# A decoder segment whose residual moves from features to tokens on the partitions

## The chip, the cores and the metric

One core of a Trainium2 chip runs the whole program. The metric is device time in microseconds (us). Five engines run side by side, each in the order of its own list of instructions, which is fixed before the run: TensorE (PE, matrix products), VectorE (DVE), ScalarE (ACT), GpSimd (POOL) and SyncE (SP). They wait for one another through semaphores. PE writes to PSUM only; DVE and ACT read PSUM and write SBUF. DMA queues bring the weights from memory.

## The reference, cut to what matters

Two layers over 256 tokens with 2048 features, all float32. Layer 0 mixes tokens with a gated recurrence (HGRN2), layer 1 with differential attention. Everything else is matrix products around one residual stream `x`:

```python
for i in range(2):
    h = rms_norm(x, ln_mix[i])
    if i == 0:
        q, f, v, g = split(h @ a_w_in)            # 2048 -> 4 * 2048
        x = x + (rms_norm(hgrn2(q, f, v), a_onorm) * silu(g)) @ a_w_out
    else:
        q = rms_norm(h @ b_w_q, q_norm)
        x = x + (rms_norm(diff_attention(q, k, v), b_subln) * c) @ b_w_out
    h = rms_norm(x, ln_mlp[i])
    x = x + square(relu(h @ mlp_up[i])) @ mlp_down[i]          # 2048 -> 8192 -> 2048
    gate = sigmoid(rms_norm(x, ln_ple[i]) @ ple_gate[i])
    x = x + gate * (p[i] @ ple_proj[i])                        # p[i]: 256 tokens, 256 features
    if i == 0:
        hk = rms_norm(x, kv_norm)
        k, v = rms_norm(hk @ w_k, k_norm), hk @ w_v
```

`rms_norm(x, gain)` divides each token's features by the root of their mean square and multiplies by a gain for each feature.

## The kernel before, in words

**Weights.** All weights stream through once, as 872 chunks of 256 rows x 512 columns (512 KB). `chunk` (lines 91 to 98) starts the transfer on SP's queue (four buffers `raw`), casts it on ACT to the first part `hi` (line 96), and subtracts on DVE to get the second part `lo` (line 97), three buffers each. A product in nearly full precision is made of three products of such parts: first by first, first by second, second by first.

**Two forms of product.** `group_b` (lines 119 to 131) makes 512 output features with the weights stationary: the activations, features on the partitions, are streamed with both their parts side by side, 2 x 256 tokens. For each 128x128 block of weights, `hi` meets 512 columns (line 114) and `lo` meets 256 columns (line 116): 16 matmuls a chunk. The result has features on the partitions and tokens along them, in two halves that are added afterwards; a group takes two of the three PSUM buffers `mm`, each two banks. `group_a` (lines 133 to 149) makes 512 output features with the tokens stationary: a 128-feature x 128-token block of the activations is loaded, and 512 columns of weights are streamed. That is 12 matmuls of 512 columns a chunk (lines 143 to 145), the result has tokens on the partitions, and a group takes one PSUM buffer. Before the change only the two value projections use `group_a`.

**Loops.** A matrix of 2048 x 2048 is four groups of eight chunks. The MLP (`mlp`, lines 518 to 543) goes in four quarters: four groups up (2048 inputs to 2048 hidden features), then four groups down from those into the residual.

**The residual.** `x` is 128 partitions x 16 blocks of features x 256 tokens: features on the partitions. After a group of the output or down projections, `add_x` (lines 242 to 245) adds both halves of each pair of blocks into it on DVE: four additions of 128x512 a group. `Norm` (lines 152 to 200) reads it: `split` multiplies each block by its gain (ACT, line 161) and forms the second part (DVE, line 162), `square` squares it on ACT and adds the squares on DVE, and `finish` sums over the partitions with a product with ones (line 189) and takes the inverse root. The scale for each token, `r`, is a row that every partition holds; for the value projections it is also turned into a column, by products with a unit vector (line 197). The scale is applied after the product that reads the norm.

**Gate and embedding.** `ple` computes the gate group by group with `group_b`, adds the halves, multiplies by `r`, takes the sigmoid in five steps, multiplies by the embedding's product `pp` and adds to `x` (lines 546 to 561). In layer 1 the last 512 features come in four blocks of 128, so that less is left after the last matmul. `Embed` makes `pp` with `group_b` from a single chunk a group: at the start for layer 0, in the second quarter of the MLP for layer 1.

**Order.** The Python code lists the instructions; side work stands in generators (`gens`), and `pump` takes one step of each after every chunk of weights. A planner of the language then fixes the order on each engine by its own costs of instructions and buffers, before the run: it takes what is ready by its own reckoning, first what was listed first. Side work of a norm is therefore two or three chunks behind the group it belongs to.

Of the kernel before, what the change touches and what calls it, by code (L numbers as in the profile page):

```python
# [14 lines left out]
ALU = mybir.AluOpType  # L15
# [13 lines left out]
# chunks of weights between a query projection and the first use of its heads  # L29
# [3 lines left out]
# columns of the packed small parameters  # L33
# [6 lines left out]
def kernel(ctx: ExitStack, tc: tile.TileContext, a):  # L40
# [32 lines left out]
    # side work in steps, one step of each after every chunk of weights  # L73
# [34 lines left out]
    def mm_b(ps, hi, lo, rhs, pair, k0, first, last):  # L108
        """out[features, 0:T] + out[features, T:2T] += w^T x, weights stationary"""
# [9 lines left out]
    def group_b(wsrc, g, rhs, evac, pump=None, c0=0, nch=NCH):  # L119
        """four blocks of features, in two pairs; the second starts once two chunks of the first are done"""  # L120
# [12 lines left out]
    def group_a(wsrc, g, xs, rcol, dst, pump=None):  # L133
        """dst[tokens, 512 features], tokens stationary"""
        ps = mm.tile([P, 2, CW], F32, tag="mm", name="mmps")
        for c in range(NCH):
            hi, lo = chunk(wsrc[g, c])
            for tt in range(2):
                ts = slice(tt * P, (tt + 1) * P)
                for k in range(KCS):  # L140
                    kc = c * KCS + k
                    st, en = kc == 0, kc == KC - 1
# [9 lines left out]
    class Norm:  # L152
        def __init__(self, src, outs):
            self.src, self.outs = src, outs
            self.ss = ev.tile([P, T], F32, tag="ss", name="ss", bufs=2)

        def split(self, g, outs=None, half=(0, 4)):
            for xs, col in outs or self.outs:
                for m in range(4 * g + half[0], 4 * g + half[1]):
                    gain = sml[:, col + m:col + m + 1]  # L160
                    nc.scalar.activation(xs[:, m, 0, :], self.src[:, m], AF.Copy, scale=gain)  # L161
                    nc.vector.scalar_tensor_tensor(xs[:, m, 1, :], self.src[:, m], gain,  # L162
                                                   xs[:, m, 0, :].bitcast(F32), ALU.mult, ALU.subtract)
# [12 lines left out]
        def spread(self, g, box=None, col=False):  # L176
            """split and square a group step by step, and, for the last one, put the scales into box"""
            for o in self.outs:
                for half in ((0, 2), (2, 4)):
                    self.split(g, [o], half)  # L180
                    yield
            self.square(g)
            yield
            if box is not None:
                yield from self.finish(box, col)

        def finish(self, box, col=False):
# [5 lines left out]
            if col:  # L193
                yield
                pc = sm.tile([P, 512], F32, tag="sm", name="smps")
                for tt in range(2):
                    nc.tensor.matmul(pc[:, 2 * tt:2 * tt + 2], r[:, tt * P:(tt + 1) * P], e0, start=True, stop=True)
                rc = ev.tile([P, 2, 2], F32, tag="rc", name="rc", bufs=2)
                nc.vector.tensor_copy(rc, pc[:, :4].rearrange("p (a b) -> p a b", a=2))
                box.append(rc)  # L200
# [11 lines left out]
    def col_sums(h):  # L212
        """sums over the partitions, on every partition"""
# [9 lines left out]
    def sigmoid(out, z, tmp):  # L223
        """1 / (1 + exp(-z)) as exp(min(z, 0) - ln(1 + exp(-|z|))), for z of any size"""
# [6 lines left out]
    def halves(ps, out):  # L231
        """out = both partial products of some feature blocks"""
# [9 lines left out]
    def add_x(m, ps):  # L242
        xm = x[:, m:m + 2]
        nc.vector.tensor_tensor(xm, ps[:, :, 0:T], xm, ALU.add)  # L244
        nc.vector.tensor_tensor(xm, ps[:, :, T:2 * T], xm, ALU.add)  # L245

    class Embed:
        """p[i] @ ple_proj[i], a group of features at a time"""
        def __init__(self, i, praw, pt):
            self.i, self.pt = i, pt  # L250
            self.pp = pq.tile([P, KC, T], F32, tag="pq", name="pp")
# [23 lines left out]
    nrm = Norm(xa, [(xs, C_MIX[0])])  # L275
# [4 lines left out]
    def start():  # L280
# [4 lines left out]
        yield from nrm.finish(RR, True)  # L285
# [3 lines left out]
    # lower bounds of the forget gates: softmax over the layers, first entry  # L289
# [524 lines left out]
```

## Time and profile before

| | us |
|---|---|
| median of 3 runs | 2550.68 |
| lowest and highest | 2545.85, 2551.82 |
| span of the profiled execution | 2545.3 |
| median of the runs less that span | 5.4 |
| PE, DVE, ACT busy in the span | 2529.0, 1686.0, 1360.0 |

The profile is of one execution; its span goes from the first to the last instruction, and its whole time isn't listed beside it. Busy times of matmuls overlap, since a matmul begins before the one ahead of it has ended; starts are what tells a rate. Granted clock 1.00 is TensorE's 2.4 GHz level.

### The profile page before, as it was taken

The numbers are of one execution on the slowest core, as the hardware profiler recorded it, in microseconds if no ns is written. First come the engines' busy times: TensorE is split into PE (matmuls) and PEld (weight loads), VectorE is DVE, ScalarE is ACT, GpSimd is POOL, SyncE is SP. The second block draws the span as 40 slices with busy tenths as digits, with TensorE's granted clock in tenths as the row PEclk, the third lists the DMA queues.
The fourth block names the chain that finished last, engine by engine and source line by source line (L and its number), as shares of the span: only waits on it lengthen the run. The fifth ranks groups of instructions, "written<-read, shape, count | busy, mean of one in ns | idle before, by whom it ended". The sixth has DMA issues, their size and how long they took to land.

```text
span 2545.3 us, 36254 instructions
## 1 busy us (share of the span) xinstructions
PE 2529.0 (99%) x14350; PEld 2199.1 (86%) x14350; DVE 1686.0 (66%) x2064; ACT 1360.0 (53%) x1703; POOL 9.7 (0%) x19
## 2 busy tenths in 40 slices
PE   8999999999999999999999999999999999999998
PEld 7888888888888888888888888888888888888887
DVE  7898887665555555556687686566555555556666
ACT  7666666444344354455576566555435445435555
POOL 0000000000000000000000000000000000000000
PEclk9999999999999999999999999999999999999999
DMA  7555554666666666666656555566666656666665
GB/s 234 173 158 166 165 174 151 214 191 189 190 189 189 187 189 190 191 189 191 183 184 186 179 154 159 169 190 185 187 183 195 185 184 197 187 188 190 190 188 159
DMA packets 128570, 467.24 MB, mean 184 GB/s; under 512 B 14288, under 2 KB 14928, under 8 KB 128400
## 3 DMA queue, kind: packets, MB, share of 16 engines
q1 hardware_dynamic: 127440, 461.95, 59.2%
q0 software_dynamic: 816, 2.89, 0.4%
q8 instruction: 112, 1.84, 0.3%
q14 instruction: 58, 0.48, 0.1%
q10 hardware_dynamic: 144, 0.09, 0.0%
HBM read 462.77 MB, written 2.10 MB: 183 GB/s over the span
## 4 chain that ended last, share of the span: by engine, by line
PE 98%; DVE 1%; DMA 0%; ACT 0%; issue 0%; SPq 0%; ACTq 0%
PE mmps L114 58%; PE mmps L116 29%; PE mmps L145 2%; PE mmps L144 2%; PE mmps L143 2%; PE smps L382 1%; PE mmps L573 1%; PE smps L216 1%; PE mmps L575 0%; DMA xa<-x_t 0%; PE smps L345 0%; PE smps L661 0%; PE smps L689 0%; DVE lo L97 0%; PE smps L413 0%; PE smps L415 0%
## 5 line engine op out<-in xcount | busy, mean ns | idle before, releaser
L114 PE MATMUL mmps<-big,hi 128*128 128x512 f32 x6336 | 2221.7, 395 | 0.1
L116 PE MATMUL mmps<-big,lo 128*128 128x256 f32 x6336 | 1770.1, 279 | 0.4 <-DVE lo L97 0.4
L97 DVE TENSOR_TENSOR lo<-raw,hi 128x1024 fp32r<-128x1024 f32 x872 | 1066.1, 1224 | 796.4 <-ACT hi L96 795.2
L96 ACT CAST hi<-raw 128x1024 fp32r<-128x1024 f32 x872 | 914.1, 1049 | 1005.9 <-PE mmps L114 926.2
L114 PEld LDWEIGHTS mmps<-big,hi 128*128 128x128 f32 x6336 | 1189.4, 188 | 278.8 <-DVE u L236 0.4
L116 PEld LDWEIGHTS mmps<-big,lo 128*128 128x128 f32 x6336 | 1191.1, 188 | 2.5 <-DVE lo L97 0.7
L143 PE MATMUL mmps<-hi,big 128*128 128x512 f32 x256 | 102.3, 399 | 0.0
L144 PE MATMUL mmps<-lo,big 128*128 128x512 f32 x256 | 100.1, 391 | 0.3 <-DVE lo L97 0.3
L145 PE MATMUL mmps<-hi,big 128*128 128x512 f32 x256 | 100.3, 392 | 0.0
L235 ACT COPY t<-mmps 128x512 f32<-128x512 f32 (+1 forms) x114 | 65.1, 572 | 24.0 <-PE mmps L116 22.3
L527 ACT ACTIVATE u<-u 128x512 f32<-128x512 f32 x64 | 40.3, 629 | 48.7 <-DVE u L526 48.7
L145 PEld LDWEIGHTS mmps<-hi,big 128*128 128x128 f32 x256 | 48.1, 188 | 10.3
L144 PEld LDWEIGHTS mmps<-lo,big 128*128 128x128 f32 x256 | 48.2, 188 | 9.7 <-DVE lo L97 0.5
L143 PEld LDWEIGHTS mmps<-hi,big 128*128 128x128 f32 x256 | 48.2, 188 | 9.1
L236 DVE TENSOR_TENSOR u<-mmps,t 128x512 f32<-128x512 f32 x80 | 54.7, 684 | 0.4
L103 DVE TENSOR_TENSOR big<-u,big 128x512 fp32r<-128x512 f32 x80 | 54.7, 683 | 0.2
L244 DVE TENSOR_TENSOR x<-mmps,x 128x512 f32<-128x512 f32 x80 | 54.5, 687 | 0.4
L102 ACT CAST big<-u 128x512 fp32r<-128x512 f32 x80 | 49.4, 618 | 4.8 <-DVE u L423 4.5
L245 DVE TENSOR_TENSOR x<-mmps,x 128x512 f32<-128x512 f32 x80 | 51.2, 680 | 0.0
L526 DVE SCALAR_TENSOR_TENSOR u<-u,rn 128x512 f32<-128x512 f32 x64 | 44.0, 688 | 1.1
L161 ACT ACTIVATE big<-x,sml 128x256 fp32r<-128x256 f32 x96 | 41.0, 498 | 6.4 <-DVE x L245 6.4
L162 DVE SCALAR_TENSOR_TENSOR big<-x,sml,big 128x256 fp32r<-128x256 f32 x96 | 40.2, 481 | 0.0
(157 smaller groups left out, 1067.6 us busy)
## 6 DMA issues: line engine op xcount, KB each, us to landing
raw<-w_up SPq DMA_DIRECT2D x256, 512.0 KB, 4.2
raw<-w_dn SPq DMA_DIRECT2D x256, 512.0 KB, 4.2
raw<-w_in SPq DMA_DIRECT2D x128, 512.0 KB, 3.7
raw<-w_pg SPq DMA_DIRECT2D x56, 512.0 KB, 3.9
raw<-w_ao SPq DMA_DIRECT2D x32, 512.0 KB, 3.8
raw<-w_k SPq DMA_DIRECT2D x32, 512.0 KB, 3.8
raw<-w_q SPq DMA_DIRECT2D x32, 512.0 KB, 3.6
raw<-w_v SPq DMA_DIRECT2D x32, 512.0 KB, 3.6
```

What stands on the lines that cost most here:

```text
L96: nc.scalar.copy(hi, raw)
L97: nc.vector.tensor_tensor(lo, raw, hi.bitcast(F32), ALU.subtract)
L103: nc.vector.tensor_tensor(dst[:, k, 1, :], src, dst[:, k, 0, :].bitcast(F32), ALU.subtract)
L114: nc.tensor.matmul(ps[:, ml, :], hi[:, k, m * P:(m + 1) * P], rhs[:, k0 + k].rearrange("p a t -> p (a t)"), start=st, stop=False)
L116: nc.tensor.matmul(ps[:, ml, T:2 * T], lo[:, k, m * P:(m + 1) * P], rhs[:, k0 + k, 0, :], start=False, stop=en)
L143: nc.tensor.matmul(ps[:, tt, :], xs[:, kc, 0, ts], hi[:, k], start=st, stop=False)
L144: nc.tensor.matmul(ps[:, tt, :], xs[:, kc, 0, ts], lo[:, k], start=False, stop=False)
L145: nc.tensor.matmul(ps[:, tt, :], xs[:, kc, 1, ts], hi[:, k], start=False, stop=en)
L235: nc.scalar.copy(t, ps[:, :, T:2 * T])
L236: nc.vector.tensor_tensor(out, ps[:, :, 0:T], t, ALU.add)
L244: nc.vector.tensor_tensor(xm, ps[:, :, 0:T], xm, ALU.add)
L245: nc.vector.tensor_tensor(xm, ps[:, :, T:2 * T], xm, ALU.add)
```

## The change

The residual becomes 128 partitions (tokens) x 2 halves of the tokens x 2048 features. Output, down and gate projections and the embedding products run in `group_a`, except the last 512 features of layer 1's gate and embedding, which stay in `group_b` form and get a copy `xl` of their residual in the old arrangement. `add_x` is two additions of 128x512 a group. A norm now takes the sum of squares along the features (ACT, with an accumulator), turns each 128x128 block of `x` with a transpose on PE into PSUM, and makes the gained parts from there. The scale for each token is now a column first; a diagonal matrix and a product with ones make the row of it. The gate's scale goes into the evacuation on ACT. The output leaves in two arrays, which the host puts together, and `x` comes from a second arrangement of the input, `x_r`, through the same four POOL transfers.

```diff
-    def group_a(wsrc, g, xs, rcol, dst, pump=None):
+    def group_a(wsrc, g, xs, evac, pump=None, c0=0, nch=NCH):
         ps = mm.tile([P, 2, CW], F32, tag="mm", name="mmps")
-        for c in range(NCH):
-            hi, lo = chunk(wsrc[g, c])
+        for c in range(nch):
+            hi, lo = chunk(wsrc[g, c0 + c])
...
-        for tt in range(2):
-            nc.scalar.activation(dst[:, tt, :], ps[:, tt, :], AF.Copy, scale=rcol[:, tt, 0:1])
+        evac(g % 4, ps)
+    def scaled_a(box, dst):
+        def evac(g, ps):
+            for tt in range(2):
+                nc.scalar.activation(dst[:, tt, :], ps[:, tt, :], AF.Copy, scale=box[1][:, tt, 0:1])
+        return evac
...
+    def gained(xs, m, src, col):
+        gain = sml[:, col + m:col + m + 1]
+        nc.scalar.activation(xs[:, m, 0, :], src, AF.Copy, scale=gain)
+        nc.vector.scalar_tensor_tensor(xs[:, m, 1, :], src, gain, xs[:, m, 0, :].bitcast(F32), ALU.mult, ALU.subtract)
+    class Norm:
...
+        def spread(self, g, box=None):
+            t = ev.tile([P, 2, T], F32, tag="t", name="t")
+            for tt in range(2):
+                nc.scalar.activation(flat(t), x[:, tt, g * CW:(g + 1) * CW], AF.Square, accum_out=self.ss[:, tt, g:g + 1])
+            yield
+            turned = []
+            for b in range(2):
+                ps = sm.tile([P, 2, T], F32, tag="sm", name="smps")
+                for i in range(2):
+                    m = 4 * g + 2 * b + i
+                    for tt in range(2):
+                        nc.tensor.transpose(ps[:, i, tt * P:(tt + 1) * P], x[:, tt, m * P:(m + 1) * P], ident)
+                turned.append(ps)
+            for xs, col in self.outs:
+                for b, ps in enumerate(turned):
+                    for i in range(2):
+                        gained(xs, 4 * g + 2 * b + i, ps[:, i], col)
+                    yield
+            if self.keep is not None and g == 3:
+                for b, ps in enumerate(turned):
+                    nc.scalar.copy(self.keep[:, 2 * b:2 * b + 2], ps)
+            if box is not None:
+                yield from self.finish(box)
+        def finish(self, box):
+            rc = ev.tile([P, 2, 1], F32, tag="rc", name="rc", bufs=2)
+            nc.vector.tensor_reduce(rc, self.ss, axis=AX.X, op=ALU.add)
+            rsqrt(rc, rc, 1.0 / D)
+            dg = ev.tile([P, T], F32, tag="rr", name="dg", bufs=1)
+            for tt in range(2):
+                nc.vector.tensor_scalar(dg[:, tt * P:(tt + 1) * P], ident, rc[:, tt, 0:1], None, ALU.mult)
+            ps = sm.tile([P, 512], F32, tag="sm", name="smps")
+            nc.tensor.matmul(ps[:, :T], ones, dg, start=True, stop=True)
+            r = ev.tile([P, T], F32, tag="rn", name="rn", bufs=2)
+            nc.scalar.copy(r, ps[:, :T])
+            box.extend((r, rc))
+            yield
...
-    def add_x(m, ps):
-        xm = x[:, m:m + 2]
-        nc.vector.tensor_tensor(xm, ps[:, :, 0:T], xm, ALU.add)
-        nc.vector.tensor_tensor(xm, ps[:, :, T:2 * T], xm, ALU.add)
+    def add_x(g, ps):
+        for tt in range(2):
+            xg = x[:, tt, g * CW:(g + 1) * CW]
+            nc.vector.tensor_tensor(xg, ps[:, tt], xg, ALU.add)
...
         def group(self, g):
-            group_b(a["w_pp"][self.i], g, self.pt, lambda m, ps: halves(ps, self.pp[:, m:m + 2]), nch=1)
+            dst = self.pp[:, :, g * CW:(g + 1) * CW]
+            if g < 4 - self.turned:
+                group_a(a["w_pp"][self.i], g, self.pt, lambda g, ps: nc.scalar.copy(dst, ps), nch=1)
+            else:
+                group_b(a["w_pp"][self.i], g, self.pt,
+                        lambda m, ps: halves(ps, dst[:, m % 4 // 2].rearrange("p (m t) -> p m t", m=2)), nch=1)
...
-    x = xp.tile([P, KC, T], F32, name="x")
+    x = xp.tile([P, 2, D], F32, name="x")
+    xl = xp.tile([P, 4, T], F32, name="xl")
     for g in range(4):
-        nc.gpsimd.dma_start(x[:, 4 * g:4 * g + 4], a["x_t"][:, 4 * g:4 * g + 4])
+        nc.gpsimd.dma_start(x[:, :, g * CW:(g + 1) * CW], a["x_r"][:, :, g * CW:(g + 1) * CW])
     def out_proj(w, rhs, xs_pool, col):
...
-            group_b(w, g, rhs, add_x, pump)
+            group_a(w, g, rhs, add_x, pump)
...
-                group_b(down, g, hid, add_x, pump, c0=NCH * qd)
+                group_a(down, g, hid, add_x, pump, c0=NCH * qd)
...
+        def chain(g, z):
+            wait = 2 if g < 3 else 0
+            gate(z)
+            for _ in range(1 + wait):
                 yield
+            gs = slice(g * CW, (g + 1) * CW)
+            nc.vector.tensor_tensor(z, z, pp[:, :, gs], ALU.mult)
+            nc.vector.tensor_tensor(x[:, :, gs], x[:, :, gs], z, ALU.add)
+            for _ in range(wait):
                 yield
-            yield from after(m, n)
+            yield from after(g)
...
+            nc.vector.tensor_tensor(xl[:, b], xl[:, b], z[:, 0], ALU.add)
+            yield
+            nc.sync.dma_start(a["out_l"][:, b], xl[:, b])
...
-            group_b(a["w_pg"][i], g, xs, lambda m, ps: halves(ps, z[:, m % 4:m % 4 + 2]), pump)
-            gens.append(chain(4 * g, 4, z))
+            group_a(a["w_pg"][i], g, xs, scaled_a(R, z), pump)
+            gens.append(chain(g, z))
```

## Rows read from the trace of the kernel before

**Rows 1.** The page's busy time of each engine, share of the span, instructions.

```profile
PE 2529.0 (99%) x14350; PEld 2199.1 (86%) x14350; DVE 1686.0 (66%) x2064; ACT 1360.0 (53%) x1703; POOL 9.7 (0%) x19
```

**Rows 2.** The page's chain that ended last, by engine.

```profile
PE 98%; DVE 1%; DMA 0%; ACT 0%; issue 0%; SPq 0%; ACTq 0%
```

**Rows 3.** Stages (start:end, length, busy us (instructions) by engine, clock, DMA share, GB/s).

```profile
608.20:697.10 88.90, 88.90 (x514) 77.68 (x513) 49.94 (x50) 36.79 (x39) 0.00 (x0) 1.00 0.64 189
...
1231.30:1322.40 91.10, 91.10 (x519) 79.08 (x518) 71.60 (x89) 62.53 (x84) 0.00 (x0) 1.00 0.61 186
...
1517.40:1622.40 105.00, 104.90 (x495) 86.27 (x494) 68.83 (x118) 64.37 (x114) 0.00 (x0) 1.00 0.51 159
...
1984.50:2086.10 101.60, 101.32 (x578) 87.84 (x577) 59.93 (x62) 45.24 (x50) 0.00 (x0) 1.00 0.61 187
```

**Rows 4.** ACT's timeline in a down projection (start us, us, instruction, [idle before, releaser]).

```profile
1000.47 1.05 ACT L96 CAST hi<-raw 128x1024 fp32r<-128x1024 f32 x1 [1.72 <-PE mmps L114]
...
1022.65 1.05 ACT L96 CAST hi<-raw 128x1024 fp32r<-128x1024 f32 x1 [1.72 <-PE mmps L114]
```

**Rows 5.** PE's timeline in the same projection.

```profile
1000.03 0.40 PE L114 MATMUL mmps<-big,hi 128*128 128x512 f32 x1
...
1000.27 0.28 PE L116 MATMUL mmps<-big,lo 128*128 128x256 f32 x1
...
1000.38 0.39 PE L114 MATMUL mmps<-big,hi 128*128 128x512 f32 x1
```

**Rows 6.** PE's timeline in the value projection of layer 1.

```profile
1600.21 0.39 PE L143 MATMUL mmps<-hi,big 128*128 128x512 f32 x1
1600.44 0.39 PE L144 MATMUL mmps<-lo,big 128*128 128x512 f32 x1
...
1605.65 0.39 PE L143 MATMUL mmps<-hi,big 128*128 128x512 f32 x1
```

**Rows 7.** PE's timeline around attention's transposes (line 679).

```profile
1526.89 0.39 PE L144 MATMUL mmps<-lo,big 128*128 128x512 f32 x1
1527.12 0.30 PE L679 MATMUL smps<-cst,L 128*128 128x128 f32 x1
1527.17 0.48 PE L145 MATMUL mmps<-hi,big 128*128 128x512 f32 x1
1527.49 0.38 PE L679 MATMUL smps<-cst,L 128*128 128x128 f32 x2
1527.62 0.48 PE L143 MATMUL mmps<-hi,big 128*128 128x512 f32 x1
1527.94 0.39 PE L144 MATMUL mmps<-lo,big 128*128 128x512 f32 x1
```

**Rows 8.** Line 679 alone: durations (ns min/median/max), and idle time before it.

```profile
L679 PE MATMUL smps<-cst,L x24: 270/273/307, 1468.2 to 1554.4; 128*128 128x128 f32 x24
...
  issue: 1.0, 4
  PE mmps L145: 0.3, 1
```

**Rows 9.** The chain that ended last, in order of time (start us, us, what).

```profile
20.07 1.23 DVE pp L236 x2
...
102.45 0.89 PE smps L382 x8
...
1991.08 1.23 DVE lo L97
1992.30 0.61 DVE u L236
```

**Rows 10.** Groups by line (engine, operation, shapes, count | busy us, mean ns | idle before).

```profile
L97 DVE TENSOR_TENSOR lo<-raw,hi 128x1024 fp32r<-128x1024 f32 x872 | 1066.1, 1224 | 796.4 <-ACT hi L96 795.2
...
L244 DVE TENSOR_TENSOR x<-mmps,x 128x512 f32<-128x512 f32 x80 | 54.5, 687 | 0.4
```

**Rows 11.** The page's DMA issues (count, size, us from issue to landing).

```profile
raw<-w_dn SPq DMA_DIRECT2D x256, 512.0 KB, 4.2
```

More of the change, by code (lines that the diff above doesn't have):

```diff
@@ L147, in group_a, with __init__, split @@
                 pump()
-        for tt in range(2):
-            nc.scalar.activation(dst[:, tt, :], ps[:, tt, :], AF.Copy, scale=rcol[:, tt, 0:1])
[L152 to L163, printed above, removed]
+        evac(g % 4, ps)
[4 more added lines that the diff above has]
+        return evac
+    class FirstNorm:
+        def __init__(self, src, xs, col):
+            self.src, self.xs, self.col = src, xs, col
+            self.ss = ev.tile([P, T], F32, tag="rn", name="ss", bufs=2)
+        def split(self, g):
+            for m in range(4 * g, 4 * g + 4):
+                gained(self.xs, m, self.src[:, m], self.col)
         def square(self, g):
@@ L174, in square @@
                         nc.vector.tensor_tensor(self.ss, self.ss, sq[:, i], ALU.add)
[L176 to L187, printed above, removed]
+        def finish(self, box):
             ps = sm.tile([P, 512], F32, tag="sm", name="smps")
@@ L192, in finish @@
             box.append(r)
[L193 to L200, printed above, removed]
+            yield
@@ L284, in start @@
             yield
-        yield from nrm.finish(RR, True)
+        yield from nrm.finish(RR)
     gens.append(start())
@@ L490, in do_v @@
             v = hg.tile([P, 2, CW], F32, tag="v", name="v", bufs=1)
-            group_a(a["w_in"], 8 + j, xs, RR[1], v, pump)
+            group_a(a["w_in"], 8 + j, xs, scaled_a(RR, v), pump)
             st[j]["v"] = v
@@ L533, in mlp @@
                 xo, box = moving(out[0]), []
-                nrm = Norm(x, [(xo, out[1])])
+                nrm = Norm([(xo, out[1])], keep)
             if qd == 1 and mid:
@@ L576, in ple @@
                     pump()
-                z = pl.tile([P, 4, T], F32, tag="pz", name="pz", bufs=2)
-                halves(ps[:, 0:1], z[:, 0:1])
-                gens.append(chain(12 + b, 1, z[:, 0:1]))
+                z = pl.tile([P, 2, CW], F32, tag="pz", name="pz", bufs=2)[:, 0:1, 0:T]
+                halves(ps[:, 0:1], z)
+                gens.append(chain_last(b, z))
             drain()
@@ L584, with feed @@
     xkv, xq = moving(s2), moving(s3)
[L585 removed]
+    nrm = Norm([(xkv, C_KV), (xq, C_MIX[1])])
     RR = []
[L588 to L589 removed]
+    def feed(g):
+        return nrm.spread(g, RR if g == 3 else None)
     ps_ = ExitStack()
@@ L716 @@
         v = at.tile([P, 2, CW], F32, tag="vb", name="vb", bufs=1)
-        group_a(a["w_v"], g, xkv, RR[1], v, pump)
+        group_a(a["w_v"], g, xkv, scaled_a(RR, v), pump)
         if g == 0:
@@ L728, in mid, with store @@
         def mid():
-            made.append(Embed(1, praw, pt))
+            made.append(Embed(1, praw, pt, 1))
             return made[0]
-        xs, R = mlp(1, xs, R, (s3, s1), (s3, C_PLE[1]), mid)
+        xs, R = mlp(1, xs, R, (s3, s1), (s3, C_PLE[1]), mid, xl)
     pp = made[0].pp
-    def store(m, n):
-        nc.sync.dma_start(a["out"][:, m:m + n], x[:, m:m + n])
+    def store(g):
+        gs = slice(g * CW, (g + 1) * CW)
+        nc.sync.dma_start(a["out"][:, :, gs], x[:, :, gs])
         yield
@@ L811 @@
     r = run_bass_kernel_spmd(nc, [arrays], core_ids=[0])
-    o = r.results[0]["out"]
-    return np.ascontiguousarray(o.transpose(1, 0, 2).reshape(D, T).T[ORDER])[None]
+    r = r.results[0]
+    o = np.concatenate([r["out"].transpose(1, 0, 2).reshape(T, D - CW), r["out_l"].transpose(2, 1, 0).reshape(T, CW)], axis=1)
+    return np.ascontiguousarray(o[ORDER])[None]
```

54 lines of the change are left out of this document (30 added, 24 removed).

## The prediction

> **What bounds the kernel now.** The first view is the page's busy time by engine [rows 1]: PE is busy for 2529.0 us of the 2545.3 us span, DVE for 66% and ACT for 53%. The chain of work that ended last agrees: 98% of it is PE [rows 2]. So an instruction costs time here when PE executes it, or when PE waits for it, and hardly otherwise. A busy PE says nothing of how fast PE is, so the second view is the order in time. In the down projections (weights stationary, `group_b`) the casts of eight successive chunks of weights are released by PE between 1000.47 and 1022.65 [rows 4], 2.773 us a chunk, and the stage row [rows 3] (first line) gives the same: 32 chunks in 88.9 us with PE busy throughout. Inside it a 512-column and a 256-column matmul take 0.35 us from start to start [rows 5], while each shows 0.40 and 0.28 as its length: lengths overlap, so the sum is made from starts. In the value projection (tokens stationary, `group_a`) 24 matmuls of 512 columns lie between 1600.21 and 1605.65 [rows 6]: 226.7 ns each.
>
> **The rate of the two forms.** A chunk in `group_b` is 8 pairs, 2.773 / 8 = 346.6 ns for 512 + 256 columns in two instructions. In `group_a` it is 12 x 512 columns, 12 x 226.7 = 2.720 us. Both stream 6144 columns. Solving 768 c + 2 f = 346.6 and 512 c + f = 226.7 gives c = 0.417 ns a column and f = 13.3 ns a matmul: 16 matmuls against 12, so 4 x 13.3 = 53 ns a chunk is what the change can win.
>
> A rule speaks against even that. The Trainium skill (TensorE: Matmul & The Clock Gate, section "Wait — 56ns, not 53.3ns?") puts the fixed cost of a warm matmul at about 2.5 ns; by that, an estimate, the gain would be 383 x 4 x 2.5 ns = 4 us and not 20, and the total some 16 us above my sum. Starts in this trace don't agree, 13.3 ns in both stages, and I go by them.
>
> **The change, part by part**, against the profiled execution's span of 2545.3 us:
>
> 1. *Chunks moved to tokens-stationary.* Two output projections 2 x 32, two down projections 2 x 128, gates 32 + 24, embeddings 4 + 3: 383 chunks x 53.3 ns = **-20.4 us**. These stages are PE-bound with room beside it: in a down projection DVE is busy 49.94 of 88.9 us and ACT 36.79 [rows 3] (first line), and the one side task that PE waits for in every chunk, `lo` (1.224 us, [rows 10]), fits into 2.72 us. Three buffers of `hi` and `lo` leave a chunk of slack. If that cover were gone, the 20.4 us would be too.
>
> 2. *Transposes.* Each of five norms (two after output projections, two after the MLPs, one after the first gate, which serves two outputs with one turn) turns 16 blocks x 2 halves: 160 transposes of 128x128 float32, 8 in a row in each of 20 places. The trace has such transposes, line 679 [rows 8]. From L144 at 1526.89 to L144 at 1527.94 [rows 7] there are three ordinary matmuls (3 x 0.227) and three transposes: 1.05 - 0.68 = 0.37, 0.123 each; the one that stands alone costs 0.143 (0.37 from it to the next, less one matmul). Eight float32 passes of 128 columns in a row take 0.89 us, 0.111 each [rows 9] (second line). Ours come in rows of eight, so nearer to that: 0.115 x 160 = **+18.4 us**. Ends: 0.143 each (22.9 us), and, if a pass ran at c and f, 128 x 0.417 + 13.3 = 67 ns (10.7 us).
>
> 3. *Norms.* `ones x ss` becomes `ones x dg`, the same float32 product of 256 columns: nothing. Of the four products that brought the scales to the partitions, two go, in two passes each: 4 x 0.111 = **-0.4 us**.
>
> 4. *Embedding in the middle of MLP 1.* That stage takes 101.6 us [rows 3] (last line) for 36 chunks worth 99.8; each embedding group takes two of three PSUM buffers, and PE waited there behind `lo` and `u` [rows 9] (last two lines). With one buffer a group, part of the 1.8 us goes: **-0.6** (0 to -1.8).
>
> 5. *Head.* The chain there runs through the embedding's two DVE adds, 1.23 us [rows 9] (first line); they become a copy on ACT. **-0.5** (-1.2 to +0.5, as the copy now queues ahead of casts on ACT).
>
> 6. *The new wait.* PE now waits for `x` in 20 places: the residual adds of a group (two of 0.687 us, [rows 10]) must be done before the transposes, and all weights' matmuls queue behind them on PE, DVE and ACT soon after. The transposes are emitted a chunk after the square, two chunks (5.4 us) behind the group's last matmul, so the adds should be long done. The eight batches on line 679, behind a longer chain, show 1.3 us of idle time before them in all [rows 8]. I take 0.05 us a place, **+1.0** (0 to 0.16 x 20 = 3.2). The tightest place is the first gate's last group, whose features are needed six chunks into the key projection, behind a stage with DVE busy 71.6 and ACT 62.5 of 91.1 us [rows 3] (second line).
>
> 7. *Off the path.* Half of the residual adds go (160 to 80), so do the multiplications of the gates by the norm and the squares' additions; the gained splits read PSUM. DVE and ACT get lighter, worth nothing by itself under PE's 98%. The residual comes through four POOL transfers as before, its first use 8 chunks (22 us) later; uncovered, one of 512 KB would cost 4.2 us [rows 11]. Weights on SP's queue keep number and size; the last store is as small as before, and the tail's chain of gate, product, addition and store has the same instructions.
>
> Sum: -20.4 + 18.4 - 0.4 - 0.6 - 0.5 + 1.0 = -2.5 us: a span of 2542.8. The median of the runs, 2550.7, lies 5.4 us over the profiled span, so the forecast is **2548 us**. With all favourable ends: -20.4 + 10.7 - 0.4 - 1.8 - 1.2 = -13 (2538); with all unfavourable: -20.4 + 22.9 - 0.4 + 0.5 + 3.2 = +6 (2556).
>
> **Rivals.**
> - *Transposes are cheaper* than their rows. At 67 ns each, 7.7 us less: 2540. For it: the matmul that starts 0.05 us after one [rows 7] (third line). Against: two in a row show 0.38 together and 0.273 each, so start 0.11 apart, and the next matmul is late by what the first seemed to save.
> - *PE waits for the residual* (the slower side). The order of each engine is fixed before the run. If it puts the transposes where the adds aren't done, PE stands with all weights' work behind them. One add, 0.687 us, in each of 20 places is 13.7 us: 2562. It decides from 0.51 us a place (10.2 us over the forecast). Against: line 679's waits.
> - *A transpose holds PE for its whole shown length*, 273 ns [rows 8]: 160 x (0.273 - 0.115) = 25 us more: 2573. Starts 0.11 us apart speak against it, and the granted clock stayed at 1.00, the 2.4 GHz level, in the stage with transposes [rows 3] (third line). The Trainium skill (same page, section "Part 4: PE-mode transpose") gives about 275 ns for one in a kernel and says that transposes don't count for the clock as other matmuls do. By that, an estimate, 160 x 275 ns = 44 us would outweigh the gain; the length agrees with the row, the holding doesn't.
> - *The change doesn't do what it says*: with `lo` late, `group_a` runs at the old 2.773 us a chunk, and the 20.4 us don't come: 2568. The same follows in part if a matmul's fixed cost is smaller than 13.3 ns; at a fifth of it, 16 us are missing: 2564. That is the Trainium skill's rule above (same page and section).
>
> **How the numbers follow.** Forecast 0.70; cheap transposes 0.14; waits over 0.51 us a place 0.10; whole length 0.03; no gain from `group_a` 0.03. About 0.3% (7.7 us: 2543 to 2558.3) is what a measurement of this kernel can tell from no change, its three runs spreading over 0.23%. Faster: the first rival and the forecast's lower edge, 0.15. Slower: the other three, 0.16. Same: 0.69. The forecast's own range is 2543 to 2556; the range goes down to 2538, where the favourable ends meet, and up to 2560, into the waits, leaving out some 0.18.
>
> **What would show it.** Starts 227 ns apart in the down projections, and 87.0 instead of 88.8 us for 32 chunks; eight transposes in about 0.9 us, 20 times; some 12,970 matmul records instead of 14,350 (-383 x 4 + 160 - 4); a mid-MLP stage under 101; no idle PE before the transposes. I'd be wrong if transposes stood 0.06 or 0.27 us apart, if PE idled half a microsecond or more before each batch, or if a down projection kept its 88.8 us.

## The result and the profile after

| | before | after |
|---|---|---|
| median (9 runs each), us | 2547.19 | 2554.68 |
| lowest to highest | 2545.46 to 2552.32 | 2553.34 to 2556.54 |
| span of the profiled execution | 2545.3 | 2554.8 |

The ratio after to before, over all runs, is 1.0025, 95% interval [1.0015, 1.0034]: slower by 0.25%. The medians alone give 0.29%, because before's runs lie in two groups, five from 2545.46 to 2547.19 and four from 2550.68 to 2552.32. The move is the other way than forecast: the sum said -2.5 us of span, the spans say +9.5. The profiled execution of after is the slowest of its nine (2556.54 us); by medians it is +7.5.

The page's busy time and its chain by engine, after, answer to [rows 1, 2]. PE's instructions fell as forecast, to 12974, DVE got lighter by 92 us, ACT stayed. By these two views alone nothing is wrong.

```profile
PE 2532.3 (99%) x12974; PEld 2151.6 (84%) x12974; DVE 1594.3 (62%) x1888; ACT 1366.1 (53%) x1743; POOL 10.3 (0%) x19
...
PE 97%; ACT 1%; DVE 1%; DMA 0%; issue 0%; SPq 0%; DVEq 0%; ACTq 0%
```

The stages, columns as in [rows 3]. The lines are a down projection of layer 0, the first gate, a down projection of layer 1, and the middle of MLP 1. The first falls from 88.90 us to 87.30, where 87.0 was forecast, and the last from 101.60 to 98.70. The third takes 89.30, two more than the first, for the same work. (These windows are cut at ACT's casts, some 5 us ahead of PE. From the stage's first matmul on PE to the next stage's first, the first line is 87.04 us, where before has 88.75, and the last is 98.34, where before has 101.66.) The first gate, which took 91.10, takes 98.90, and PE stands for 4.28 us of it at a mean clock of 0.97. Two of the three places of the loss are there.

```profile
607.10:694.40 87.30, 87.30 (x394) 72.59 (x393) 46.49 (x44) 37.10 (x38) 0.00 (x0) 1.00 0.59 193
...
1228.00:1326.90 98.90, 94.62 (x411) 77.06 (x410) 59.44 (x66) 61.77 (x89) 0.00 (x0) 0.97 0.52 170
...
1814.80:1904.10 89.30, 89.30 (x394) 72.79 (x393) 46.50 (x44) 36.96 (x39) 0.00 (x0) 1.00 0.58 189
...
1994.30:2093.00 98.70, 98.70 (x446) 81.86 (x446) 52.65 (x50) 44.90 (x47) 0.00 (x0) 1.00 0.59 192
```

Short windows around two of the three places at which PE stands, in the gate (1284 to 1291) and just behind it, at the start of the key projection (1338 to 1346). In the first row of each pair PE is busy for 1.26 of 3.40 us and 1.99 of 3.70; in the second it is busy throughout, but the granted clock is 0.51, the 1.2 GHz level. The place between (1311) shows the same as the first.

```profile
1284.00:1287.40 3.40, 1.26 (x5) 0.48 (x4) 2.94 (x5) 3.40 (x5) 0.00 (x0) 1.00 0.01 2
1287.50:1291.00 3.50, 3.50 (x9) 2.72 (x10) 3.50 (x4) 1.12 (x2) 0.00 (x0) 0.51 0.73 235
...
1338.40:1342.10 3.70, 1.99 (x10) 1.20 (x9) 3.56 (x4) 3.70 (x6) 0.00 (x0) 1.00 0.00 0
1342.10:1345.60 3.50, 3.50 (x13) 2.96 (x13) 3.50 (x4) 0.99 (x2) 0.00 (x0) 0.51 0.89 262
```

PE's timeline there (start, length, instruction, idle before it and what ended it). The eight transposes of line 216 run at 1275.42 without any wait. Some nine microseconds later PE idles twice: for `hi`, from ACT's cast, and then for `lo`, from DVE. By starts (0.227 us for a matmul) the two waits hold it for 1.31 + 1.26 = 2.58 us. Behind them matmuls start 0.42 us apart, at the lower clock.

```profile
1275.42 1.03 PE L216 MATMUL smps<-cst,x 128*128 128x128 f32 x8
1276.21 0.49 PE L143 MATMUL mmps<-hi,big 128*128 128x512 f32 x1
...
1284.29 0.39 PE L145 MATMUL mmps<-hi,big 128*128 128x512 f32 x1
1285.83 0.50 PE L143 MATMUL mmps<-hi,big 128*128 128x512 f32 x1 [1.15 <-ACT hi L96]
1287.32 0.62 PE L144 MATMUL mmps<-lo,big 128*128 128x512 f32 x1 [0.99 <-DVE lo L97]
1287.74 0.63 PE L145 MATMUL mmps<-hi,big 128*128 128x512 f32 x1
1288.16 0.63 PE L143 MATMUL mmps<-hi,big 128*128 128x512 f32 x1
```

So the question is why ACT's cast was late, and ACT's own timeline answers it. Between the cast at 1275.62 and the one at 1284.70 it makes none for 9 us, in which PE, at 2.72 us a chunk, uses up the three chunks of lead that three buffers give. But for 0.95 us behind DVE, ACT isn't waiting in that time, it is working: the first gained splits that follow the transposes (L195), the evacuation of the next group's product (L154), then the gate's sigmoid (L267 to L269) and the other splits in turn.

```profile
1275.62 1.05 ACT L96 CAST hi<-raw 128x1024 fp32r<-128x1024 f32 x1 [1.67 <-PE mmps L145]
1276.57 0.83 ACT L195 ACTIVATE big<-smps,sml 128x256 fp32r<-128x256 f32 x2
1278.35 0.87 ACT L195 ACTIVATE big<-smps,sml 128x256 fp32r<-128x256 f32 x2 [0.95 <-DVE big L196]
1279.28 1.27 ACT L154 ACTIVATE pz<-mmps,rc 128x512 f32<-128x512 f32 x2
1280.43 0.48 ACT L195 ACTIVATE big<-smps,sml 128x256 fp32r<-128x256 f32 x1
1280.79 1.07 ACT L267 ACTIVATE pt<-pz 128x1024 f32<-128x1024 f32 x1
...
1283.40 1.08 ACT L269 ACTIVATE pt<-pt 128x1024 f32<-128x1024 f32 x1
1284.35 0.49 ACT L195 ACTIVATE big<-smps,sml 128x256 fp32r<-128x256 f32 x1
1284.70 2.02 ACT L96 CAST hi<-raw 128x1024 fp32r<-128x1024 f32 x2
```

The splits could have run earlier. DVE's timeline has the addition that makes the group's `x` ready, done at 1268.6, nearly 7 us before the transposes:

```profile
1267.39 1.22 DVE L605 TENSOR_TENSOR x<-x,pz 128x1024 f32<-128x1024 f32 x1
```

In the kernel before, the same split had no PE instruction ahead of it: it read `x` itself. ACT's timeline of before in the gate's stage shows a cast, one step of the sigmoid, a cast, and six splits in a row (L161) between two casts.

```profile
1286.46 1.05 ACT L96 CAST hi<-raw 128x1024 fp32r<-128x1024 f32 x1 [0.67 <-PE mmps L114]
1287.42 1.06 ACT L225 ACTIVATE pt<-pz 128x1024 f32<-128x1024 f32 x1
1288.38 1.03 ACT L96 CAST hi<-raw 128x1024 fp32r<-128x1024 f32 x1
...
1296.35 1.05 ACT L96 CAST hi<-raw 128x1024 fp32r<-128x1024 f32 x1 [1.60 <-PE mmps L114]
1297.38 2.51 ACT L161 ACTIVATE big<-x,sml 128x256 fp32r<-128x256 f32 x6
1299.79 1.04 ACT L96 CAST hi<-raw 128x1024 fp32r<-128x1024 f32 x1
```

From these views the theory: a PE that is never free has no gap in its list into which the planner could move the transposes, so they stay where the code lists them. `chain` yields three steps before the product (one, and the two of `wait`) and two behind the addition, and the square one more, so six steps go by. A step is taken after each chunk, the first of them after the next group's first chunk, so the transposes stand behind the seventh of that group's eight chunks, that is, just before its evacuation and sigmoid are due, and all the work that needs their result lands on ACT at once. Three groups wait like this (`wait = 2 if g < 3`), and there are three places. The waits hold 2.58 + 2.58 + 2.04 = 7.2 us by starts, and three stretches of about 3.4 us at half speed cost 1.7 us each, 5.1. Without these 12.3 us the span of this execution would be 2542.5; the sum had said 2542.8.

### The profile page after: what moved, and what is told of

It reads as the page before. It is cut to its first block, busy times and chain, and to the rows that moved or that the text cites. A ratio compares the mean times of both kernels' runs of the same rounds, so it can differ in the third digit from the quotient of the medians.

```text
span 2554.8 us, 33339 instructions
## 1 busy us (share of the span) xinstructions
PE 2532.3 (99%) x12974; PEld 2151.6 (84%) x12974; DVE 1594.3 (62%) x1888; ACT 1366.1 (53%) x1743; POOL 10.3 (0%) x19
## 4 chain that ended last, share of the span: by engine, by line
PE 97%; ACT 1%; DVE 1%; DMA 0%; issue 0%; SPq 0%; DVEq 0%; ACTq 0%
PE mmps L114 30%; PE mmps L144 16%; PE mmps L145 16%; PE mmps L143 16%; PE mmps L116 16%; PE smps L429 1%; PE smps L216 1%; PE smps L258 1%; PE mmps L630 1%; DVE lo L97 0%; PE mmps L632 0%; DMA xa<-x_t 0%; PE smps L392 0%; PE smps L718 0%; PE smps L746 0%; ACT big L195 0%
## 5 line engine op out<-in xcount | busy, mean ns | idle before, releaser
L114 PE MATMUL mmps<-big,hi 128*128 128x512 f32 x3328 | 1173.9, 396 | 0.9 <-ACT hi L96 0.9
L116 PE MATMUL mmps<-big,lo 128*128 128x256 f32 x3328 | 937.1, 282 | 0.9 <-DVE lo L97 0.9
L114 PEld LDWEIGHTS mmps<-big,hi 128*128 128x128 f32 x3328 | 625.0, 188 | 144.0 <-ACT hi L96 1.3
L143 PE MATMUL mmps<-hi,big 128*128 128x512 f32 x1760 | 693.1, 394 | 2.3 <-ACT hi L96 2.3
L144 PE MATMUL mmps<-lo,big 128*128 128x512 f32 x1760 | 689.3, 392 | 2.3 <-DVE lo L97 2.3
L145 PE MATMUL mmps<-hi,big 128*128 128x512 f32 x1760 | 689.1, 392 | 0.0
L116 PEld LDWEIGHTS mmps<-big,lo 128*128 128x128 f32 x3328 | 628.4, 189 | 3.4 <-DVE lo L97 1.8
L143 PEld LDWEIGHTS mmps<-hi,big 128*128 128x128 f32 x1760 | 331.6, 188 | 72.4 <-ACT hi L96 3.1
L144 PEld LDWEIGHTS mmps<-lo,big 128*128 128x128 f32 x1760 | 331.7, 188 | 72.0 <-DVE lo L97 3.1
L145 PEld LDWEIGHTS mmps<-hi,big 128*128 128x128 f32 x1760 | 331.5, 188 | 71.1 <-DVE big L103 0.3
L287 DVE TENSOR_TENSOR x<-mmps,x 128x512 f32<-128x512 f32 x80 | 51.6, 686 | 17.1 <-PE mmps L145 17.1
L195 ACT ACTIVATE big<-smps,sml 128x256 fp32r<-128x256 f32 x96 | 41.6, 474 | 19.5 <-DVE big L196 18.0
L196 DVE SCALAR_TENSOR_TENSOR big<-smps,sml,big 128x256 fp32r<-128x256 f32 x96 | 42.6, 479 | 13.0 <-ACT big L195 12.8
```

Source lines behind the costliest of these rows:

```text
L114: nc.tensor.matmul(ps[:, ml, :], hi[:, k, m * P:(m + 1) * P], rhs[:, k0 + k].rearrange("p a t -> p (a t)"), start=st, stop=False)
L116: nc.tensor.matmul(ps[:, ml, T:2 * T], lo[:, k, m * P:(m + 1) * P], rhs[:, k0 + k, 0, :], start=False, stop=en)
L143: nc.tensor.matmul(ps[:, tt, :], xs[:, kc, 0, ts], hi[:, k], start=st, stop=False)
L144: nc.tensor.matmul(ps[:, tt, :], xs[:, kc, 0, ts], lo[:, k], start=False, stop=False)
L145: nc.tensor.matmul(ps[:, tt, :], xs[:, kc, 1, ts], hi[:, k], start=False, stop=en)
L287: nc.vector.tensor_tensor(xg, ps[:, tt], xg, ALU.add)
```

## The experiments

The span is that of one profiled execution; the ratio is to runs of the kernel before on the same chip.

| | span | median | ratio to before [95%] |
|---|---|---|---|
| e1, no waiting steps | 2543.3 | 2545.17 | 0.9989 [0.9980, 0.9998] |
| e2, evacuation on DVE | 2542.7 | 2544.41 | 0.9988 [0.9979, 0.9997] |
| e3, banks in turn | 2551.3 | 2554.43 | 1.0025 [1.0016, 1.0034] |
| e4, each transpose twice | 2562.1 | 2563.92 | 1.0062 [1.0047, 1.0077] |
| e5, transposes early | 2546.2 | 2547.81 | 1.0000 [0.9991, 1.0009] |
| e6, e1 and e2 | 2543.6 | 2545.56 | 0.9993 [0.9985, 1.0002] |
| e7, e1, other buffers in layer 1 | 2538.4 | 2540.20 | 0.9970 [0.9959, 0.9981] |
| e8, before with e7's buffers | 2546.4 | 2547.33 | 1.0000 [0.9991, 1.0008] |
| e9, e1, other buffers in layer 0 | 2547.5 | 2549.01 | 1.0011 [1.0001, 1.0021] |
| e10, before once more | 2543.3 | 2545.05, one run | |

**e1: the transposes follow their group at once.**

```diff
         def chain(g, z):
-            wait = 2 if g < 3 else 0
+            wait = 0
```

> The changed kernel, but the gate's chain of a group waits no further steps (wait = 0 for every group instead of 2), so the residual is updated after one step and the norm's transposes stand some four chunks earlier in PE's list. Theory (position): PE is never idle, so it keeps to the list and the transposes stand where they were listed, six chunks into the next group; the gained splits they feed then meet the next group's evacuation and sigmoid on ACT, no cast gets through for 9 us, PE waits 2.0 to 2.6 us at each of three group ends and then runs at half clock for 3.41 us. Moved, all three waits and all three stretches at 1.2 GHz go: span 2554.8 - 7.2 - 5.1 = 2542.5 us, ratio to before 0.998 to 0.9995. Rival (the evacuation on ACT with the scale is what is too much, wherever the splits stand): the waits stay, span 2553 to 2555, ratio 1.002 to 1.0035.

All three waits are gone, and with them the low clock. The span of 2543.3 is 11.5 below that of after's profiled execution, of the 12.3 that its rows price; by medians the gain is 9.5 us. The kernel is faster than before by 0.1%, by medians by 0.06%. PE's timeline of e1 has the same transposes 6.5 us earlier:

```profile
1268.94 1.06 PE L216 MATMUL smps<-cst,x 128*128 128x128 f32 x8
1269.76 0.49 PE L143 MATMUL mmps<-hi,big 128*128 128x512 f32 x1
```

On ACT the casts now stand between the splits and the evacuation, and the gate's stage takes 91.70 us at clock 1.00, PE busy throughout (the two fences are ACT's timeline and the stage's window):

```profile
1270.21 0.82 ACT L195 ACTIVATE big<-smps,sml 128x256 fp32r<-128x256 f32 x2
1271.60 1.04 ACT L96 CAST hi<-raw 128x1024 fp32r<-128x1024 f32 x1
1274.19 1.06 ACT L96 CAST hi<-raw 128x1024 fp32r<-128x1024 f32 x1 [0.81 <-PE mmps L145]
...
1279.63 1.27 ACT L154 ACTIVATE pz<-mmps,rc 128x512 f32<-128x512 f32 x2 [1.30 <-PE mmps L145]
1280.79 1.05 ACT L96 CAST hi<-raw 128x1024 fp32r<-128x1024 f32 x1
```

```profile
1228.20:1319.90 91.70, 91.70 (x419) 75.52 (x418) 60.93 (x70) 63.85 (x94) 0.00 (x0) 1.00 0.55 184
```

**e2: the position stays, the gate's evacuation goes to DVE.**

```diff
+            for tt in range(2):
+                nc.vector.tensor_scalar(dst[:, tt, :], ps[:, tt, :], box[1][:, tt, 0:1], None, ALU.mult)
...
-            group_a(a["w_pg"][i], g, xs, scaled_a(R, z), pump)
+            group_a(a["w_pg"][i], g, xs, scaled_dve(R, z), pump)
```

> The changed kernel, but the gate's product leaves PSUM with its scale on DVE and not on ACT; transposes and splits stay where they are. Theory (position): the stretch without a cast on ACT gets shorter by the two evacuations (1.27 us) and by what else slips behind a cast, so the waits shrink from 2.6 to about 1 us or less and the low clock may or may not follow: span 2543 to 2549, ratio 0.9985 to 1.001. Rival (the evacuation on ACT is the cause by itself): the waits go entirely, as in the run without waiting steps: 2542 to 2543.

Better than the theory expected: no wait is left at all. With 1.27 us less on ACT a cast slips in between the splits, at 1279.37 in ACT's timeline of e2 (L202 is after's L195), and that one is enough:

```profile
1278.40 0.87 ACT L202 ACTIVATE big<-smps,sml 128x256 fp32r<-128x256 f32 x2 [0.95 <-DVE big L203]
1279.37 1.06 ACT L96 CAST hi<-raw 128x1024 fp32r<-128x1024 f32 x1
```

So the collision needs both the late position and the evacuation beside it. That either edit alone removes the loss also means that e1 and e2 don't say which of the two to blame; e5 does.

**e3: are the splits slow because ACT and DVE meet in PSUM?** ACT's splits wait 18.0 us in all for DVE's (L195 for L196) in the trace of after. The edit makes them take the two banks in turn.

```diff
-                for b, ps in enumerate(turned):
-                    for i in range(2):
+                for i in range(2):
+                    for b, ps in enumerate(turned):
```

> The changed kernel, but the gained splits take the two PSUM tiles of a turned group in turn instead of one after the other. In the changed kernel ACT waits 18.0 us in all for DVE's split, as if both could not read one PSUM tile in two following splits. Rival (the splits read one tile and ACT and DVE take turns): these 18 us go, each stretch without a cast gets 1 to 3 us shorter, the waits of PE shrink to 0 to 1.5 us, ratio 0.999 to 1.001. Theory (position): what fills ACT is the sum of splits, evacuation and sigmoid; with at most 1 us saved a wait of 1.5 us or more stays at each of the three ends and with it the low clock: span 2550 to 2555, ratio 1.001 to 1.0035.

The rival falls: the waits of ACT for DVE remain (18.1 us), PE's waits remain, and the median is that of after. The windows right behind its three waits brought something else. In this one execution only the second was followed by the lower clock, and its span is 3.5 us shorter than after's: two stretches at half speed, 2 x 1.7. The waits price themselves, then, and the clock is a second price that is paid in some executions and not in others; the runs of after and of e3 spread over 3 and 5 us, those of e1 over 0.6. The mean granted clock of e3's eleven runs goes with their times: three at 0.999 took 2551.31 to 2553.45 us, five at 0.998 took 2553.26 to 2555.12, three at 0.997 took 2556.32 to 2556.44.

```profile
1287.50:1291.00 3.50, 3.50 (x17) 2.86 (x16) 3.50 (x4) 1.96 (x2) 0.00 (x0) 1.00 0.68 228
...
1313.20:1316.70 3.50, 3.50 (x11) 2.72 (x9) 3.50 (x4) 0.62 (x1) 0.00 (x0) 0.51 0.80 246
...
1339.90:1343.40 3.50, 3.50 (x22) 3.08 (x21) 3.50 (x4) 1.95 (x2) 0.00 (x0) 1.00 0.75 260
```

**e4: what does a transpose cost?** Each is issued twice.

```diff
-                        nc.tensor.transpose(ps[:, i, tt * P:(tt + 1) * P], x[:, tt, m * P:(m + 1) * P], ident)
+                        for _ in range(2):
+                            nc.tensor.transpose(ps[:, i, tt * P:(tt + 1) * P], x[:, tt, m * P:(m + 1) * P], ident)
```

> The changed kernel with each of the 160 transposes issued twice into the same place. It prices them by themselves. Forecast's price (0.115 us each, read as 0.87 us for eight in a row afterwards): +17.4 to +18.4 us over the changed kernel, span 2572 to 2574, ratio 1.009 to 1.010. Rivals: 0.067 us each, span 2565.5; their whole shown length of 0.273 us, span 2598.

The expected total was missed: 7.3 us of span above after, because the longer rows of transposes moved ACT's order too, and of the waits only two of 0.72 us and one of 0.28 were left, at full clock. Taken against e1, which has no waits, it is 18.8 us, 1.7 of them waits, so 160 more transposes cost 17.1, 0.107 us each. PE's timeline of e4 gives nearly the same directly: sixteen take 1.66 us from the first's start to the next matmul's, where eight take 0.79 (after, at 1275.42), so eight more cost 0.87, 0.109 each or 17.4 for 160. The window of that stage is at clock 1.00; from first matmul to next stage's first it takes 96.99 us against 94.41 in after.

```profile
459.26 1.91 PE L217 MATMUL smps<-cst,x 128*128 128x128 f32 x16
460.92 0.48 PE L143 MATMUL mmps<-hi,big 128*128 128x512 f32 x1
```

```profile
421.20:519.10 97.90, 97.90 (x469) 81.09 (x469) 53.27 (x58) 50.41 (x69) 2.84 (x4) 1.00 0.59 194
```

**e5: the waiting steps stay listed, but the transposes are given priority in the planner's order.** This separates the position on PE from the waiting steps.

```diff
-                        nc.tensor.transpose(ps[:, i, tt * P:(tt + 1) * P], x[:, tt, m * P:(m + 1) * P], ident)
+                        with tc.high_priority():
+                            nc.tensor.transpose(ps[:, i, tt * P:(tt + 1) * P], x[:, tt, m * P:(m + 1) * P], ident)
```

> The changed kernel with one thing changed: the transposes get a higher priority in the planner, so PE takes them as soon as the residual is ready by its reckoning; the gate's waiting steps, the squares, the splits and the evacuation on ACT stay as listed. Theory (PE, never idle, keeps to the list, and the late transposes push the splits onto the next group's evacuation and sigmoid): the transposes move by some four chunks, casts stand between the splits again, all three waits of 2.0 to 2.6 us and the stretches at 1.2 GHz go: span 2542 to 2544, ratio 0.998 to 0.9998, as in the run without waiting steps. Rival (the waiting steps in the gate's chain delay its last product and addition, and that is what hurts): the chain still waits, so the waits stay: 2551 to 2555.

The gate's waits are gone with the steps left in place, which puts the loss on the transposes' position. The total is 2.9 us above e1's, more than expected: 16 of the 20 rows of eight now come in two pieces with a matmul between, and the stages with norms are 0.1 to 0.6 us longer, some 2 us in all; what the rest is isn't shown. PE's timeline at one of them:

```profile
455.00 0.44 PE L217 MATMUL smps<-cst,x 128*128 128x128 f32 x2
455.19 0.49 PE L144 MATMUL mmps<-lo,big 128*128 128x512 f32 x1
...
455.75 0.82 PE L217 MATMUL smps<-cst,x 128*128 128x128 f32 x6
```

**e6: e1 and e2 together.**

```diff
-            wait = 2 if g < 3 else 0
+            wait = 0
...
-            group_a(a["w_pg"][i], g, xs, scaled_a(R, z), pump)
+            group_a(a["w_pg"][i], g, xs, scaled_dve(R, z), pump)
```

> No waiting steps, and the gate's product leaves PSUM on DVE: both cures at once. Theory: with either of them no wait of PE is left, so the second finds nothing to gain: span 2542 to 2543.5, ratio 0.998 to 0.9995, equal to each alone within 1 us. Rival (each took away half of the cost by another way): 2537 to 2540.

No better than either alone, so both take away the same thing and no further wait was behind it.

**e7: the two microseconds of a down projection of layer 1.** In after, the stages whose stationary operand lies in the buffer `s3` (two down projections and the gate of layer 1) run 232.4 ns a matmul, the others 226.7. To e1 is added an exchange of `s3` and `s2` in layer 1, so that `s3` holds only operands that are streamed (in the up projections).

```diff
-    xs, R = out_proj(a["w_bo"], O, s2, C_MLP[1])
+    xs, R = out_proj(a["w_bo"], O, s3, C_MLP[1])
...
-        xs, R = mlp(1, xs, R, (s3, s1), (s3, C_PLE[1]), mid, xl)
+        xs, R = mlp(1, xs, R, (s2, s1), (s2, C_PLE[1]), mid, xl)
```

> No waiting steps, and in layer 1 the third activation buffer (s3) and the second (s2) change places: norms after the mixer in s3, hidden features of the MLP in s2 and s1, the gate's input in s2. In the changed kernel the tokens-stationary stages that read s3 take 232.4 ns a matmul (first and third down quarter of layer 1, its gate), the others 226.7; all executions agree to 0.1 ns. Theory (the rate goes with the buffer that the stationary operand lies in): all three stages drop to 226.7 ns, -2.2, -2.2 and -1.6 us, the up projections may move by 1 us either way: span 2536 to 2539, ratio 0.996 to 0.9975. Rival (the rate goes with the stage, by its place in the program or its weights): 232.4 stays in these stages, span 2542.5 to 2544.

The three stages fall to 226.8 ns a matmul, 5.9 us in all, and the span by 4.9 us below e1's: of the up projections of layer 1, which now stream from `s3`, two got 1.0 and 1.1 us longer and two 0.6 shorter. The windows of the first down projection and of the gate of layer 1 take 87.40 and 66.70 us, where after takes 89.30 and 68.10. At 2540.20 us, 0.30% below before, this version beats both kernels.

```profile
1804.20:1891.60 87.40, 87.40 (x395) 72.65 (x394) 46.47 (x44) 37.12 (x38) 0.00 (x0) 1.00 0.59 193
...
2436.30:2503.00 66.70, 66.70 (x299) 55.29 (x299) 39.49 (x39) 39.48 (x50) 0.00 (x0) 1.00 0.61 202
```

**e8: the same exchange in the kernel before**, where this operand is streamed and not stationary.

```diff
-    xs, R = out_proj(a["w_bo"], O, s2, C_MLP[1])
+    xs, R = out_proj(a["w_bo"], O, s3, C_MLP[1])
...
-        xs, R = mlp(1, xs, R, (s3, s1), (s3, C_PLE[1]), mid)
+        xs, R = mlp(1, xs, R, (s2, s1), (s2, C_PLE[1]), mid)
```

> The kernel before with the same change of buffers in layer 1 and nothing else. Theory (the rate goes with the buffer): its weights-stationary stages on s3, at 353.3, 348.9 and 353.3 ns a pair, drop towards 346.7: -1.7, -0.6 and -1.3 us, ratio 0.998 to 0.9995. Rival (with the stage): unchanged, 0.9995 to 1.0005.

No gain in the total, though much moved. Of the three stages that left `s3`, the two down quarters fell as the theory had it (353.3 and 348.9 to 346.7 ns a pair of matmuls), the gate stayed at 353; three up projections that now stream from `s3` rose from 346.7 to 348.9. But stages of layer 0 moved as much, where the edit changes neither PE's list nor an address: 352.9 to 346.8 in the output projection, 353.3 to 347.4 in the gate, 348.9 to 353.3 in three up projections. So the buffer alone doesn't set the rate of weights-stationary stages; whether it has a part in it is open.

**e9: the mirror image of e7**, in layer 0: to e1 is added that two down projections and the gate take their stationary operand from `s3`.

```diff
-    xs, R = out_proj(a["w_ao"], O, s3, C_MLP[0])
-    xs, R = mlp(0, xs, R, (s1, s2), (s1, C_PLE[0]))
+    xs, R = out_proj(a["w_ao"], O, s1, C_MLP[0])
+    xs, R = mlp(0, xs, R, (s3, s2), (s3, C_PLE[0]))
```

> No waiting steps, and in layer 0 the activation buffers change places so that the tokens-stationary stages of its first and third down quarter and of its gate read s3 instead of s1 (norm after the mixer in s1, hidden features in s3 and s2, the gate's input in s3; the query's input in s1 and the keys in s3). Layer 1 is as in the changed kernel. Theory (the rate of tokens-stationary matmuls goes with the buffer): these three stages go from 226.7 to 232.4 ns, +2.2, +2.2 and +2.2 us, span 2548 to 2551, ratio 1.0008 to 1.002. Rival (it goes with the stage or with the program as a whole): they stay at 226.7, span 2541 to 2545.

The three stages go to 232.3 to 232.4 ns, the down projection from after's 87.30 to 89.30 us and the gate from e1's 91.70 to 93.10 (windows of e9). The span of 2547.5 is 0.5 below the range expected. For tokens-stationary stages the buffer decides, in both layers and both directions.

```profile
606.40:695.70 89.30, 89.30 (x394) 72.82 (x394) 46.50 (x44) 36.99 (x38) 0.00 (x0) 1.00 0.57 189
...
1231.60:1324.70 93.10, 93.10 (x419) 75.97 (x418) 61.29 (x71) 63.46 (x95) 0.00 (x0) 1.00 0.55 181
```

**e10: the kernel before in a second profiled execution**, to see what of its rates belongs to the execution; nothing is edited.

> The kernel before once more, for the rates of its stages in another execution. If a stage's rate is a matter of the program, all stages agree with the first trace within 0.2 ns a pair (layer 0's up quarters 348.8, its output projection 352.9, layer 1's first down quarter 353.3). If it is a matter of the execution, some stages stand at another of the levels 346.7, 348.8, 351 and 353.3.

Part does. The first down projection of layer 1, the same instructions of the same program, takes 90.50 us in the first trace and 89.30 in this one. The two stages ahead of it moved too, by +1.2 and -1.3 us (from first matmul to first matmul); the other quarters of the MLPs agree within 0.02 us:

```profile
1805.10:1895.60 90.50, 90.50 (x514) 78.74 (x514) 49.99 (x50) 36.65 (x39) 0.00 (x0) 1.00 0.61 186
```

```profile
1804.30:1893.60 89.30, 89.30 (x514) 78.20 (x514) 50.00 (x50) 36.64 (x38) 0.00 (x0) 1.00 0.63 189
```

## Why the prediction was wrong

**Step 6 failed, together with step 7.** Step 6 looked at one wait that the change adds, PE for `x`, and priced it right: the transposes of line 216 show no idle time before them, and `x` was ready 7 us early. But it put all transposes two chunks behind their group: the diff has six steps for three of the gate's four groups. And it stopped at the transposes. What stands behind them, eight splits on ACT and DVE, depends on where PE runs them, and the step didn't ask what ACT has to do at that point: it named the first gate's last group as the tightest place for PE's wait, in the right stage, with the wrong victim. Step 7 then called the lighter DVE and ACT "worth nothing" either way, by their sums; ACT is at 53% and still has 9 us without a cast in three places. In place of the 1.0 us of step 6 the change brought 7.2 us of waits for `hi` and `lo`, and 5.1 us at the low clock behind them, in the profiled execution. The cover of step 1 ("three buffers of `hi` and `lo` leave a chunk of slack") was the cover that went. The waiting steps of `chain` are in the diff, and chunk counts from it put the splits on the next group's evacuation: the step's own working, carried one engine further, leads there.

**The rivals.** None had the mechanism. *PE waits for the residual* came nearest in size but has the wrong wait; *`lo` late* had the right wait, spread over 383 chunks rather than at three group ends. *Cheap transposes* and *a transpose holds PE* both fall to e4.

**Step 2, the transposes: right, a little high.** 0.107 to 0.109 us each, some 17.4 us, for 0.115 and 18.4. Each shows 272 ns. The Trainium skill (TensorE: Matmul & The Clock Gate, "Part 4: PE-mode transpose") gives about 275 ns for one in a kernel, measured in bf16, and says that they don't engage the fast clock. The length agrees, but in a row one costs 0.109 us. The clock stayed at 1.00 in stages with eight and with sixteen in a row; no run here has transposes without matmuls around them.

**Step 1, the rate: right in the form it was derived from, not everywhere.** The first three down quarters of layer 0 take 87.0 to 87.1 us from first matmul to the next stage's first, for 87.0 (87.3 to 87.4 in windows). The Trainium skill's fixed cost of about 2.5 ns a warm matmul (same page, "Wait — 56ns, not 53.3ns?") would have taken 32 x 4 x 2.5 ns = 0.3 us off them, an estimate, where 1.7 went: the trace stays with the 13.3 ns. Unforeseen were 6.0 us (2.2 + 2.2 + 1.6) in the three stages with `s3`. On the other side the stages of before were not all at the 346.6 ns of [rows 4, 5] either: the one in e10's comparison ran at 353.3. Between e1 and before, without waits, everything but the transposes came to -2.0 - 17.4 = -19.4 us where steps 1, 3, 4 and 5 promised -21.9; the 2.5 between them is about what two executions of the kernel before differ by (2.0). That the sum comes so near is in part luck. From first matmul to first matmul, five up projections that the change leaves alone take 0.55 to 1.7 us longer in e1 than in before, 5.0 in all, and `s3` cost 6.0; against them four converted stages of before stood near 353 ns a pair (output projection and gate of layer 0, first down quarter and gate of layer 1), so each gave 1.3 to 1.7 us more than step 1 counts.

**Steps 3 to 5: nothing against them, and little that tests them.** The middle of MLP 1 is at 98.70, forecast under 101; of its 2.9 us, 35 chunks x 53.3 ns = 1.9 belong to step 1, and 1.0 is left for step 4 (1.5 by PE's starts), forecast 0.6. PE reaches the first output projection 0.5 to 1.1 us earlier than in before's trace and 0.1 to 0.7 earlier than in e10's; step 5 forecast 0.5, and that its copy is the reason isn't shown. Step 3 is too small to be told apart.

**From span to median.** The 5.4 us that were added were mostly the accident of three runs. In every run of the record the time is 1.7 to 1.9 us above the span of the same run. By that the forecast would have read 2544.6; e1, the change without the three waits, has 2545.17.

Not tried: a fourth buffer of `hi` and `lo`, which would test the chunks of lead themselves.

## What to carry to other kernels

When a step is moved onto the engine that is never idle, it stays at its place in the list, here until it was given priority (e5), and so does all that follows it: count in chunks where its successors land, and add up, engine by engine, what else is due there between two items that the busy engine needs. An engine at 53% can be late for 9 us; the check is the longest stretch without a cast against the lead that the buffers hold, not the share of busy time. And a wait on a busy TensorE has two prices, the idle time and the slower matmuls behind it (7.2 us and 5.1 in after's profiled execution); the second isn't paid in every execution.

## What was unexpected of the hardware

- Behind waits of 2.58, 2.58 and 2.04 us, each in two parts, PE's next matmuls ran for about 3.4 us at 0.51, in three places of three in after's execution. In e3's, behind waits of 2.56, 2.55 and 2.00 us, they did so in one of three: the length of the wait alone doesn't tell.
- Matmuls of 512 columns with the tokens stationary take 226.7 ns from start to start when the stationary operand lies in `s1` or `s2` and 232.4 in `s3` (e7, e9). What of that buffer does it is open.
- Weights-stationary pairs run at levels between 346.7 and 353.3 ns, mostly one level to a stage, for the same form of instruction; which level a stage has can change from one execution of one program to the next (e10). Its cause is open.
